# The last output group on one Trainium2 core: both token halves share the first k-tiles, and the accumulators come from another pool

## The chip, the cores and the metric

The kernel runs on one core of one Trainium2 chip. The metric is the device time of one execution in microseconds, as the median of several runs. The profile is that of one more execution; its span is what the profiler saw of it from the first to the last event.

## The reference

One layer of a decoder trunk with three token-mixer branches. What matters here is its end:

```python
merged = (g_sb * (o_sb @ w_branch_sb[layer])
          + g_ssd * (o_ssd @ w_branch_ssd[layer])
          + g_mem * (o_mem @ w_branch_mem[layer]))
x = x + merged @ w_out[layer]
...
return rms_norm(x, final_norm_w)
```

`x` is 256 tokens by 2048 channels in float32, `w_out` is 2048 by 2048. The final norm divides each token's row by the root of the mean of its squares, so no part of a row can be written before all 2048 columns of it are there.

## The kernel before

**Tiles.** The 256 tokens are two halves of 128 (`t` is 0 or 1); the 2048 output columns are four groups of `GW` = 512 (`g` is 0 to 3); the contraction over 2048 is 16 k-tiles of 128 (`NKT`). The transposed `merged` lies in `mT` as a high and a low part (`lh`, `ll`), and each chunk of the weights is split in the same manner: ScalarE rounds `raw` to a high part (line 146), VectorE subtracts that for the low part (line 150). A product is then three matmuls: high by high, high by low, low by high.

**Order.** The instructions of each engine stand in the order in which the program is written; a heap of deferred functions (`defer`, `pump`, `drain`) only decides where in that order the evacuations are written. Each engine works its queue in order and waits at semaphores for the others. The framework sets these waits: for data, and for a buffer of a pool whose former tile has not been read yet.

**The groups 0 to 2** go through `gemm`: an accumulator of two banks (one for each token half) from the pool `psA`, which has two such buffers; chunks of two k-tiles; evacuation by `out_half` (VectorE adds `x`, ScalarE squares and sums, GpSimd multiplies by the norm's weights).

**The group 3** is written out by hand. All its weights are loaded and split first, into tiles that stay (`wlh`, `wll`); then `drain()` writes what is still deferred, among it the evacuation of group 2; then come the products, half 0 in one piece of 512 columns, half 1 in two pieces of 256 (`T`), each piece with its own accumulator:

```python
acc = psA.tile([P, 2, GW], F32, tag="acc", name=nm("acc"),
               bufs=2)[:, 0, 0:cs.stop - cs.start]
...
last_cols(t, cs, acc, xr[:, t])
```

`last_cols` goes over 256 columns at a time: VectorE adds `x` (line 891), ScalarE squares and sums (895), VectorE adds the sum to the row's mean (896) and multiplies by the norm's weights (897). Behind the last columns of a half, `write_out` takes the power -1/2 on GpSimd (901), scales the row in five pieces, three on VectorE (908) and two on ScalarE (910), and sends each piece off (911) on the queue of SyncE or of ScalarE.

**The other pool.** `bank(...)` gives single banks of the pool `psB`, which has four buffers. In this part of the program it last held the transposes of `merged` (`mt`, line 832).

Of the kernel before, what the change touches and what calls it, by code (L numbers as in the profile page):

```python
# [10 lines left out]
F32 = mybir.dt.float32  # L11
# [5 lines left out]
P = 128  # L17
D = 2048
T = 256
NKT = D // P  # L20
GW = 512
# [4 lines left out]
LATE = 3  # L26
WARM = 10
LATE_C = 2
NEG = -1.0e30

SB_HEADS = 8
# [10 lines left out]
def trunk_kernel(  # L42
# [6 lines left out]
    nc = tc.nc  # L49
# [7 lines left out]
    psA = ctx.enter_context(tc.tile_pool(name="psA", bufs=2, space=bass.MemoryType.PSUM))  # L57
# [4 lines left out]
    def nm(s):  # L62
        cnt[0] += 1
        return f"{s}_{cnt[0]}"
# [13 lines left out]
    def tq(shape, n):  # L78
        return tmp.tile(shape, F32, tag="tq", name=nm(n), bufs=2)

    def small(shape, n="small"):
        return sm.tile(shape, F32, tag="small", name=nm(n), bufs=12)
# [4 lines left out]
    def bank(shape, n="bank"):  # L87
        return psB.tile(shape, F32, tag="bank", name=nm(n))
# [19 lines left out]
    def keep_warm(n):  # L108
        for _ in range(n):
# [9 lines left out]
    nc.gpsimd.memset(cmask, 0.0)  # L119
    nc.gpsimd.affine_select(out=smask, in_=cmask, compare_op=ALU.is_gt, fill=NEG, base=0,  # L120
                            pattern=[[1, P]], channel_multiplier=-1)
    nc.gpsimd.affine_select(out=cmask, in_=cmask, compare_op=ALU.is_ge, fill=NEG, base=0,
                            pattern=[[1, P]], channel_multiplier=-1)
# [48 lines left out]
    def defer(fn, chunks=LATE):  # L172

        cnt[0] += 1
        heapq.heappush(late, (now[0] + chunks, cnt[0], fn))
# [9 lines left out]
    def pump():  # L185


        now[0] += 1
        while late and late[0][0] <= now[0]:
            heapq.heappop(late)[2]()  # L190
        advance(lanes[now[0] % 2])
# [6 lines left out]
    def drain():  # L198
        while lanes[0] or lanes[1] or late:
            pump()  # L200
# [10 lines left out]
    def gemm_cols(lhs, nk, w, c0, evac, ready=None, acc=None):  # L211
# [7 lines left out]
        for k0 in range(0, nk, KCC):  # L219
# [16 lines left out]
            pump()  # L236
        defer(lambda: evac(acc), LATE_C)

# [200 lines left out]
    for g in range(4):  # L439
        gemm_cols(memT, NKT, w_mem_kv, 2 * g * P, to_split_cols(kT, 2 * g),  # L440
                  acc=None if g else [bank([P, 2, T], "acc") for _ in range(2)])
# [384 lines left out]
    mT = []  # L826
# [61 lines left out]
    def last_cols(t, cs, acc, xr):  # L888
        for c in range(cs.start, cs.stop, T):
            yc = yo[t][:, 3 * GW + c:3 * GW + c + T]  # L890
            nc.vector.tensor_tensor(yc, acc[:, c - cs.start:c - cs.start + T], xr[:, c:c + T],
                                    ALU.add)
            junk = tq([P, T], "junk")
            q = ssy[:, t, 3 + c // T:4 + c // T]
            nc.scalar.activation(junk, yc, AF.Square, scale=D ** -0.5, accum_out=q)
            nc.vector.tensor_tensor(msy[:, t:t + 1], q, msy[:, t:t + 1], ALU.add)
            nc.vector.tensor_tensor(yc, yc, fw[:, 3 * GW + c:3 * GW + c + T], ALU.mult)

    def write_out(t):
        rs = small([P, 1], "frs")  # L900
        nc.gpsimd.tensor_tensor(rs, msy[:, t:t + 1], mhalf[:, 0:1], ALU.pow)
        for c0, c1, eng, dma in ((0, 256, nc.vector, nc.sync), (256, 640, nc.scalar, nc.scalar),
                                 (640, 1152, nc.vector, nc.sync),
                                 (1152, 1536, nc.scalar, nc.scalar),
                                 (1536, 2048, nc.vector, nc.sync)):
            o = yo[t][:, c0:c1]
            if eng is nc.vector:
                eng.tensor_scalar(o, o, rs, None, ALU.mult)
            else:
                eng.activation(o, o, AF.Copy, scale=rs)  # L910
            dma.dma_start(out[t * P:(t + 1) * P, c0:c1], o)

    def x_chunk(g):
        xr = t4([P, 2, GW], "xr")
        nc.scalar.dma_start(
            xr, x[:, g * GW:(g + 1) * GW].rearrange("(t p) n -> p t n", p=P))
        return xr
# [9 lines left out]
        gemm(mT[0], NKT, w_out, g * GW, out_evac(g))  # L927


    g = 3  # L930
    xr = x_chunk(g)
    his, los = [], []
# [4 lines left out]
        raw = load_chunk(w_out, g * GW, GW, k0, KC)  # L937
        split((his[-1][:, k0 % 4:k0 % 4 + KC], los[-1][:, k0 % 4:k0 % 4 + KC], raw, None))
    drain()
    for t in range(2):  # L940
        tt = slice(t * P, (t + 1) * P)
        for cs in (slice(0, GW),) if t == 0 else (slice(0, T), slice(T, GW)):
            acc = psA.tile([P, 2, GW], F32, tag="acc", name=nm("acc"),
                           bufs=2)[:, 0, 0:cs.stop - cs.start]
            for kt in range(NKT):
                lh, ll = mT[0].at(kt)
                wh, wl = his[kt // 4][:, kt % 4, cs], los[kt // 4][:, kt % 4, cs]
                nc.tensor.matmul(acc, lh[:, tt], wh, start=(kt == 0), stop=False)
                nc.tensor.matmul(acc, lh[:, tt], wl, start=False, stop=False)
                nc.tensor.matmul(acc, ll[:, tt], wh, start=False, stop=(kt == NKT - 1))  # L950
            last_cols(t, cs, acc, xr[:, t])
        write_out(t)


_INS = ['x', 'mem', 'x_cols', 'mem_cols', 'w_cols', 'w_in', 'b_gate', 'dt_bias', 'a_log',
# [39 lines left out]
```

## Time and profile before

| what | value |
|---|---|
| median of 3 runs | 1228.92 us |
| lowest and highest | 1228.18 and 1229.08 us |
| the profiled execution | 1229.58 us |
| its span | 1227.9 us |
| first product of group 3 | 1196.19 us from the span's start |
| last product's end | 1219.84 us |

The profiled execution takes 1.68 us more than its span; that is what lies around the profiled part. Matmuls are pipelined: their starts are closer together than one of them lasts, so the distance between starts is their pace.

### The profile page before, as it was taken

To read this page: it belongs to the slowest core of one execution; us is meant where nothing else is said; L and a number is where in the kernel's file an instruction comes from. 1 tells how busy PE (TensorE), PEld (TensorE's weight loads), DVE (VectorE), ACT (ScalarE), POOL (GpSimd) and SP (SyncE) were. 2 spreads that over 40 slices of the span, in tenths; PEclk is the share of its full clock that TensorE was granted. 3 is DMA by queue.
4 is the path that set the end of the run, shared out by engine and by line. 5 is a ranking of instruction groups with operands and counts; after the bars stand their busy time and mean duration, and the time that the engine had idled before them with its cause. 6 is when DMAs were issued, how large, how long until landed. Compare 5 with 4: busy or idle time off the path is not lost.

```text
span 1227.9 us, 16571 instructions
## 1 busy us (share of the span) xinstructions
PE 1215.4 (99%) x6388; PEld 1034.5 (84%) x6388; DVE 784.5 (64%) x990; ACT 646.0 (53%) x873; POOL 50.9 (4%) x50
## 2 busy tenths in 40 slices
PE   9999999999999999999999999999999999999997
PEld 7888888888888888888888888888878888888886
DVE  5686654565654555888878758577677655555554
ACT  6765444554445454545664756474757544444443
POOL 0000000000000000010100000000000010110101
PEclk9999999999999999999999999999999999999999
DMA  9966566655566656556567666676756666567673
GB/s 333 349 197 188 163 194 189 186 169 166 162 185 181 183 173 187 171 174 179 179 183 225 206 198 219 175 225 188 223 186 186 208 191 210 184 199 242 201 239 112
DMA packets 175023, 242.70 MB, mean 198 GB/s; under 512 B 10272, under 2 KB 109792, under 8 KB 174816
## 3 DMA queue, kind: packets, MB, share of 16 engines
q1 hardware_dynamic: 168224, 229.51, 61.0%
q10 hardware_dynamic: 6720, 12.13, 2.8%
q8 instruction: 50, 0.82, 0.3%
q14 instruction: 29, 0.24, 0.1%
HBM read 239.48 MB, written 2.13 MB: 197 GB/s over the span
## 4 chain that ended last, share of the span: by engine, by line
PE 94%; DMA 2%; ACT 2%; DVE 1%; issue 1%; SPq 0%; POOLq 0%; POOL 0%; ACTq 0%
PE acc L229 29%; PE acc L233 14%; PE acc L266 14%; PE acc L267 14%; PE acc L268 14%; PE acc L398 1%; PE acc L399 1%; PE acc L397 1%; PE y L772 1%; DMA raw<-in_w_branch_sb_dram 1%; DMA raw<-in_w_out_dram 1%; ACT wh L146 1%; DMA raw<-in_w_mem_kv_dram 1%; DVE wl L150 0%; ACT dec L752 0%
## 5 line engine op out<-in xcount | busy, mean ns | idle before, releaser
L150 DVE TENSOR_TENSOR wl<-raw,wh 128x1024 fp32r<-128x1024 f32 (+1 forms) x409 | 504.7, 1237 | 311.3 <-ACT wh L146 305.7
L146 ACT ACTIVATE wh<-raw 128x1024 fp32r<-128x1024 f32 (+1 forms) x409 | 431.1, 1055 | 392.7 <-PE acc L268 200.7
L229 PE MATMUL acc<-hT,wh 128*128 128x512 f32 x1408 | 444.0, 397 | 0.0
L233 PEld LDWEIGHTS acc<-hT,wl 128*128 128x128 f32 x1408 | 264.5, 188 | 62.5
L233 PE MATMUL acc<-hT,wl 128*128 128x256 f32 x1408 | 276.8, 278 | 0.0
L229 PEld LDWEIGHTS acc<-hT,wh 128*128 128x128 f32 x1408 | 214.5, 189 | 0.1
L267 PE MATMUL acc<-wl,hT 128*128 128x512 f32 x448 | 174.8, 390 | 1.4 <-DVE wl L150 1.4
L266 PE MATMUL acc<-wh,hT 128*128 128x512 f32 x448 | 175.8, 392 | 0.0
L268 PE MATMUL acc<-wh,hT 128*128 128x512 f32 x448 | 174.5, 390 | 0.0
L267 PEld LDWEIGHTS acc<-wl,hT 128*128 128x128 f32 x448 | 84.1, 188 | 19.3 <-DVE wl L150 2.3
L266 PEld LDWEIGHTS acc<-wh,hT 128*128 128x128 f32 x448 | 84.1, 188 | 17.7 <-issue 0.7
L268 PEld LDWEIGHTS acc<-wh,hT 128*128 128x128 f32 x448 | 84.1, 188 | 17.6
L266 PE MATMUL acc<-wh,oD 128*128 128x512 f32 x128 | 49.8, 389 | 0.0
L267 PE MATMUL acc<-wl,oD 128*128 128x512 f32 x128 | 49.8, 389 | 0.0
L268 PE MATMUL acc<-wh,oD 128*128 128x512 f32 x128 | 49.8, 389 | 0.0
L687 DVE SCALAR_TENSOR_TENSOR cT<-cu,wcols,cT 128x255 f32<-128x255 f32 (+2 forms) x96 | 46.4, 483 | 3.4
L852 POOL TENSOR_TENSOR merged<-merged,sig 128x512 f32<-128x512 f32 x16 | 24.8, 1572 | 523.7 <-DVE sig L851 523.7
L229 PE MATMUL acc<-memT,wh 128*128 128x512 f32 x128 | 40.5, 398 | 0.0
L266 PE MATMUL acc<-wh,mT 128*128 128x512 f32 x96 | 37.4, 390 | 0.0
L268 PE MATMUL acc<-wh,mT 128*128 128x512 f32 x96 | 37.4, 389 | 0.0
L267 PE MATMUL acc<-wl,mT 128*128 128x512 f32 x96 | 37.4, 389 | 0.0
L630 POOL TENSOR_TENSOR lm<-lm,sp 128x384 f32<-128x384 f32 x8 | 13.1, 1638 | 394.7 <-DVE sp L629 385.0
(250 smaller groups left out, 1297.3 us busy)
## 6 DMA issues: line engine op xcount, KB each, us to landing
raw<-in_w_in_dram SPq DMA_DIRECT2D x288, 512.0 KB, 3.7
raw<-in_w_branch_ssd_dram SPq DMA_DIRECT2D x32, 512.0 KB, 4.1
raw<-in_w_out_dram SPq DMA_DIRECT2D x32, 512.0 KB, 4.9
raw<-in_w_mem_kv_dram SPq DMA_DIRECT2D x31, 512.0 KB, 6.0
raw<-in_w_branch_mem_dram SPq DMA_DIRECT2D x16, 512.0 KB, 3.6
raw<-in_w_branch_sb_dram SPq DMA_DIRECT2D x16, 512.0 KB, 4.9
dec<-acT SPq DMA_DIRECT2D x24, 256.0 KB, 7.7
sig<-in_b_gate_dram ACTq DMA_DIRECT2D x12, 256.0 KB, 4.3
```

Of the source, the lines that this page charges most:

```text
L146: nc.scalar.activation(hi, src, AF.Copy, **({} if scale is None else {"scale": scale}))
L150: nc.vector.tensor_tensor(lo, src, h32, ALU.subtract)
L229: nc.tensor.matmul(halves[b], wh[:, kt - k0, b * P:(b + 1) * P], lhs.both(kt), start=first, stop=False, skip_group_check=True)
L233: nc.tensor.matmul(halves[b][:, 1], wl[:, kt - k0, b * P:(b + 1) * P], lhs.at(kt)[0], start=False, stop=last, skip_group_check=True)
L266: nc.tensor.matmul(a, lh[:, tt], wh[:, j], start=first, stop=False)
L267: nc.tensor.matmul(a, lh[:, tt], wl[:, j], start=False, stop=False)
L268: nc.tensor.matmul(a, ll[:, tt], wh[:, j], start=False, stop=last)
L397: nc.tensor.matmul(a, lh[:, tt], wh[:, g], start=first, stop=False)
L398: nc.tensor.matmul(a, lh[:, tt], wl[:, g], start=False, stop=False)
L630: nc.gpsimd.tensor_tensor(lm, lm, sp, ALU.subtract)
L687: nc.vector.scalar_tensor_tensor(a[:, s:T], u[:, 0:T - s], convw[:, 3 - s, i:i + 1], a[:, s:T], ALU.mult, ALU.add)
L852: nc.gpsimd.tensor_tensor(merged[t][:, cs], merged[t][:, cs], sig[:, t], ALU.add)
```

## The change

Group 3's products are written in another order, and both accumulators are taken from the pool `psB`, one bank of 512 columns for each token half. For the first 8 k-tiles (`BOTH`) the three matmuls of half 0 are followed by the three of half 1, 512 columns each. Then half 0 does its k-tiles 8 to 15, and `last_cols` and `write_out` of half 0 are written. Then half 1 does its k-tiles 8 to 15 for columns 0 to 255, `last_cols` of these, the same for columns 256 to 511, and `write_out`. Nothing else of the kernel is touched; its lines stand one lower.

```diff
+BOTH = 8
...
     drain()
-    for t in range(2):
+
+    accs = [bank([P, GW], "acc") for _ in range(2)]
+
+    def products(t, cs, k0, k1, ends=False):
         tt = slice(t * P, (t + 1) * P)
-        for cs in (slice(0, GW),) if t == 0 else (slice(0, T), slice(T, GW)):
-            acc = psA.tile([P, 2, GW], F32, tag="acc", name=nm("acc"),
-                           bufs=2)[:, 0, 0:cs.stop - cs.start]
-            for kt in range(NKT):
-                lh, ll = mT[0].at(kt)
-                wh, wl = his[kt // 4][:, kt % 4, cs], los[kt // 4][:, kt % 4, cs]
-                nc.tensor.matmul(acc, lh[:, tt], wh, start=(kt == 0), stop=False)
-                nc.tensor.matmul(acc, lh[:, tt], wl, start=False, stop=False)
-                nc.tensor.matmul(acc, ll[:, tt], wh, start=False, stop=(kt == NKT - 1))
-            last_cols(t, cs, acc, xr[:, t])
-        write_out(t)
+        for kt in range(k0, k1):
+            lh, ll = mT[0].at(kt)
+            wh, wl = his[kt // 4][:, kt % 4, cs], los[kt // 4][:, kt % 4, cs]
+            for i, (a, b) in enumerate(((lh, wh), (lh, wl), (ll, wh))):
+                nc.tensor.matmul(accs[t][:, cs], a[:, tt], b, start=(kt == 0 and i == 0),
+                                 stop=(ends and kt == k1 - 1 and i == 2),
+                                 skip_group_check=True)
+
+    everything = slice(0, GW)
+    for kt in range(BOTH):
+        for t in range(2):
+            products(t, everything, kt, kt + 1)
+    products(0, everything, BOTH, NKT, ends=True)
+    last_cols(0, everything, accs[0], xr[:, 0])
+    write_out(0)
+    for cs in (slice(0, T), slice(T, GW)):
+        products(1, cs, BOTH, NKT, ends=True)
+        last_cols(1, cs, accs[1][:, cs], xr[:, 1])
+    write_out(1)
```

How TensorE's order changes at the start of group 3. The rows give line, operation, output and inputs, the output's partitions by columns, and in brackets the engine for whose semaphore the instruction waits. Before, with `acc_10153` for half 0:

```order
L948 MATMUL acc_10153<-wlh_10099,mT_8525 128x512 [waits Activation_49]
L949 MATMUL acc_10153<-wll_10100,mT_8525 128x512 [waits DVE_49]
L950 MATMUL acc_10153<-wlh_10099,mT_8525 128x512
L948 MATMUL acc_10153<-wlh_10099,mT_8525 128x512
L949 MATMUL acc_10153<-wll_10100,mT_8525 128x512
L950 MATMUL acc_10153<-wlh_10099,mT_8525 128x512
```

And of the change, with `acc_10153` for half 0 and `acc_10154` for half 1:

```order
L951 MATMUL acc_10153<-wlh_10099,mT_8525 128x512 [waits PE_49,Activation_49]
L951 MATMUL acc_10153<-wll_10100,mT_8525 128x512 [waits DVE_49]
L951 MATMUL acc_10153<-wlh_10099,mT_8525 128x512
L951 MATMUL acc_10154<-wlh_10099,mT_8525 128x512 [waits PE_49]
L951 MATMUL acc_10154<-wll_10100,mT_8525 128x512
L951 MATMUL acc_10154<-wlh_10099,mT_8525 128x512
```

Half 1's first products moved up between those of half 0; their waits for TensorE itself are for writes in these banks that lie some 440 products back.

TensorE again, where columns 0 to 255 of half 1 end and columns 256 to 511 begin. Before, in two accumulators (`acc_10224`, `acc_10278`):

```order
L948 MATMUL acc_10224<-wlh_10129,mT_8528 128x256
L949 MATMUL acc_10224<-wll_10130,mT_8528 128x256
L950 MATMUL acc_10224<-wlh_10129,mT_8528 128x256
L948 MATMUL acc_10278<-wlh_10099,mT_8525 128x256 [waits DVE_49,PE_49]
L949 MATMUL acc_10278<-wll_10100,mT_8525 128x256
L950 MATMUL acc_10278<-wlh_10099,mT_8525 128x256
```

And of the change, both in `acc_10154`:

```order
L951 MATMUL acc_10154<-wlh_10129,mT_8528 128x256 x2
L951 MATMUL acc_10154<-wll_10130,mT_8528 128x256
L951 MATMUL acc_10154<-wlh_10129,mT_8528 128x256
L951 MATMUL acc_10154<-wlh_10119,mT_8527 128x256 [waits DVE_49]
L951 MATMUL acc_10154<-wll_10120,mT_8527 128x256
```

The wait before was for the first readers of `acc_10153`, whose buffer `acc_10278` takes; that of the change is for another VectorE instruction, the addition of half 1 that stands fourth in the next rows (the number that the wait names is the one that this addition counts up to).

VectorE's order in the change, from `write_out(0)` into `last_cols(1)` (`yo_9616` is the output row block of half 0, `yo_9617` that of half 1):

```order
L909 TENSOR_SCALAR yo_9616<-yo_9616,frs_10237 128x256 [waits Pool_49]
L909 TENSOR_SCALAR yo_9616<-yo_9616,frs_10237 128x512
L909 TENSOR_SCALAR yo_9616<-yo_9616,frs_10237 128x512 [waits DVE_49]
L892 TENSOR_TENSOR yo_9617<-acc_10154,xr_10097 128x256 [waits PE_49]
L897 TENSOR_TENSOR msy<-ssy,msy 128x1 [waits Activation_49]
L898 TENSOR_TENSOR yo_9617<-yo_9617,fw_9618 128x256 [waits DVE_49]
L892 TENSOR_TENSOR yo_9617<-acc_10154,xr_10097 128x256 [waits PE_49]
```

Nothing moved on VectorE: the same instructions stand in the same order before, with the accumulators `acc_10224` and `acc_10278` in the two additions.

## Rows read from the trace of the kernel before

**Rows 1.** From the page: the span, TensorE's busy time, and the chain that ended last by engine.

```profile
span 1227.9 us, 16571 instructions
PE 1215.4 (99%) x6388; PEld 1034.5 (84%) x6388; DVE 784.5 (64%) x990; ACT 646.0 (53%) x873; POOL 50.9 (4%) x50
...
PE 94%; DMA 2%; ACT 2%; DVE 1%; issue 1%; SPq 0%; POOLq 0%; POOL 0%; ACTq 0%
```

**Rows 2.** Who waited for whom from 1185 to 1228 us: us in total, times, longest.

```profile
DVE yo L891 <- PE acc L950: 4.6, 2, 4.2
...
PEld acc L948 <- DVE yo L879: 1.2, 1, 1.2
...
PE acc L948 <- DVE yo L879: 0.8, 1, 0.8
```

**Rows 3.** Timeline of TensorE (PE) in group 3: start, us, line, output and inputs, shape; the idle time before it in brackets. The first and last of half 0 (48 products of 512 columns), the first two of half 1's columns 0 to 255, its last (the 48th), and the last of columns 256 to 511.

```profile
1196.19 0.39 PE L948 MATMUL acc<-wlh,mT 128*128 128x512 f32 x1
...
1206.86 0.39 PE L950 MATMUL acc<-wlh,mT 128*128 128x512 f32 x1
...
1208.06 0.39 PE L948 MATMUL acc<-wlh,mT 128*128 128x256 f32 x1 [0.81 <-DVE yo L879]
...
1208.29 0.28 PE L949 MATMUL acc<-wll,mT 128*128 128x256 f32 x1
...
1213.80 0.28 PE L950 MATMUL acc<-wlh,mT 128*128 128x256 f32 x1
...
1219.56 0.28 PE L950 MATMUL acc<-wlh,mT 128*128 128x256 f32 x1
```

**Rows 4.** Timeline: the last subtraction for `wll` on VectorE (DVE), and the product of half 0 that reads it.

```profile
1204.45 1.22 DVE L150 TENSOR_TENSOR wll<-raw,wlh 128x1024 fp32r<-128x1024 f32 x1 [0.45 <-ACT wlh L146]
...
1205.95 0.40 PE L949 MATMUL acc<-wll,mT 128*128 128x512 f32 x1
```

**Rows 5.** Timeline of VectorE: the last two instructions of group 2's evacuation shown are the addition for half 1 and the mean's step; then `last_cols(0)`, the three scalings of `write_out(0)` merged into one row, and the first addition of half 1.

```profile
1207.33 0.68 DVE L879 TENSOR_TENSOR yo<-acc,xr 128x512 f32<-128x512 f32 x1
...
1208.99 0.15 DVE L886 TENSOR_SCALAR msy<-fs 128x1 f32<-128x1 f32 x1
1209.07 0.42 DVE L891 TENSOR_TENSOR yo<-acc,xr 128x256 f32<-128x256 f32 x1
...
1210.21 0.42 DVE L897 TENSOR_TENSOR yo<-yo,fw 128x256 f32<-128x256 f32 x1
1210.54 0.42 DVE L891 TENSOR_TENSOR yo<-acc,xr 128x256 f32<-128x256 f32 x1
...
1212.55 1.14 DVE L908 TENSOR_SCALAR yo<-yo,frs 128x256 f32<-128x256 f32 x3 [0.45 <-POOL frs L901]
1214.12 0.42 DVE L891 TENSOR_TENSOR yo<-acc,xr 128x256 f32<-128x256 f32 x1 [0.43 <-PE acc L950]
```

**Rows 6.** Timeline of the other engines there: the power on GpSimd (POOL), ScalarE's (ACT) second output transfer of half 0, its square of half 1's columns 0 to 255, and VectorE's steps behind it.

```profile
1211.84 0.67 POOL L901 TENSOR_TENSOR frs<-msy,mhalf 128x1 f32<-128x1 f32 x1 [1.70 <-DVE msy L896]
...
1214.25 0.36 ACTq L911 DMA_DIRECT2D out_dram<-yo  x1
...
1214.66 0.42 ACT L895 ACTIVATE junk<-yo 128x256 f32<-128x256 f32 x1 [0.44 <-DVE yo L891]
...
1215.20 0.16 DVE L896 TENSOR_TENSOR msy<-ssy,msy 128x1 f32<-128x1 f32 x1 [0.65 <-ACT junk L895]
...
1215.28 0.42 DVE L897 TENSOR_TENSOR yo<-yo,fw 128x256 f32<-128x256 f32 x1
```

**Rows 7.** Timeline of the tail: the last addition, and the last output transfer that is issued.

```profile
1219.88 0.42 DVE L891 TENSOR_TENSOR yo<-acc,xr 128x256 f32<-128x256 f32 x1 [4.18 <-PE acc L950]
...
1223.51 0.34 ACTq L911 DMA_DIRECT2D out_dram<-yo  x1
```

**Rows 8.** Stretches: two that hold most of group 3's products, then single microseconds behind the last of them. Columns: length, busy us of PE, PEld, DVE, ACT, POOL (with counts), then TensorE's granted clock as a share of full speed, the DMA engines' busy share and GB/s.

```profile
1196.19:1207.25 11.06, 11.06 (x49) 8.82 (x47) 7.34 (x8) 5.75 (x7) 0.14 (x1) 1.00 0.44 152
...
1213.82:1219.84 6.02, 6.02 (x51) 5.82 (x49) 0.92 (x3) 0.91 (x3) 0.00 (x0) 1.00 0.50 176
...
1220.00:1221.00 1.00, 0.00 (x0) 0.00 (x0) 0.42 (x3) 0.51 (x2) 0.00 (x0) 1.00 0.00 0
...
1223.00:1224.00 1.00, 0.00 (x0) 0.00 (x0) 0.00 (x0) 0.47 (x1) 0.00 (x0) 1.00 0.95 338
1224.00:1225.00 1.00, 0.00 (x0) 0.00 (x0) 0.00 (x0) 0.00 (x0) 0.00 (x0) 0.66 1.00 384
```

**Rows 9.** The DMA engines' busy share, in tenths, from 1190 to 1228 us in 40 slices of 0.95 us. Slices 25 to 28 (from 1213.7) are the output of half 0, slices 34 to 37 (from 1222.3) that of half 1, counted from 0.

```profile
DMA  8997579869793000000000000999100000199800
```

## The prediction

> **What bounds the kernel now.** I read the page first, then the waits of the last 43 us, then the timeline of the last group engine by engine. The page shows one engine as the limit: TensorE is busy for 99% of the span and stands for 94% of the chain that ended last [rows 1]. Only the last 32 us differ between the two kernels, so the views are narrowed to them. Of the waits there, one is TensorE's own: 0.81 us before the first product of token half 1 (the last two rows of the group) [rows 2]. Everything behind TensorE's last product is a serial tail: VectorE's addition of the last quarter starts at 1219.88 and the span ends at 1227.9 [rows 1, 7], 8.02 us in which TensorE does nothing. What counts for the end of the program is therefore one moment: when VectorE begins that last addition (the second `last_cols` of token half 1, columns 256 to 511). Whatever the change does, I take the 8.02 us behind it as they are, and ask where that moment moves.
>
> **Where it lies now.** TensorE does 48 products of 512 columns for half 0: the first starts at 1196.19, the last at 1206.86, so one starts every (1206.86 - 1196.19)/47 = 0.227 us. It then stands until 1208.06, and does 96 products of 256 columns, one every 0.12 us from there on (1213.80 to 1219.56 is 48 of them, 5.76 us). The last ends at 1219.56 + 0.28 = 1219.84 [rows 3], and VectorE starts 0.04 us behind it [rows 7].
>
> **What the change takes away.** Two things on TensorE. First the stand. `acc` of half 1 came out of a pool of two buffers, and the one it was given had still to be read by VectorE for group 2 (the addition at 1207.33, which ends at 1208.01) [rows 2, 5]. The new accumulators are in the other pool, whose buffers were last read by splits of `mT` long before; neither of them waits for group 2. From the pace, the next product would have stood at 1206.86 + 0.227 = 1207.09 rather than 1208.06, so this is 0.97 us. Second, 48 products of 256 columns become 24 of 512: 48 x 0.12 - 24 x 0.227 = 5.76 - 5.45 = 0.31 us. Taken by TensorE alone, the last product would then start at 1196.19 + 72 x 0.227 + 47 x 0.12 = 1218.17 and end at 1218.45: 1.39 us earlier than now.
>
> **What it costs nothing to move.** In the new order each pair of k-tiles is used at a slower pace at first (both halves use it), so the weights have more time. Before, the last subtraction that makes a `wll` ends at 1204.45 + 1.22 = 1205.67 and the product that reads it started at 1205.95 [rows 4]; now the same tile is wanted after 48 + 19 products, at 1196.19 + 67 x 0.227 = 1211.4. The cover is 5.7 us, and the splits themselves wait for loads and for nothing that TensorE does here. The additions, squares and multiplications of group 2 (`out_half`) stay where they were, behind the splits on VectorE, until 1209.1 [rows 5]; nothing of the last group waits for them any more.
>
> **What it moves later, and this is the dear part.** Half 0 now ends not after 48 products but after 72. The last starts at 1196.19 + 71 x 0.227 = 1212.31, ends 0.39 later, and with the same 0.04 VectorE's first addition of half 0 starts at 1212.74 instead of 1209.07: 3.67 us later. Behind it on VectorE stand, in this order and before anything of half 1, the rest of `last_cols(0)` and the three scalings of `write_out(0)`. From the first addition to the first scaling is 1212.55 - 1209.07 = 3.48 us (squares on ScalarE and the power on GpSimd lie in between), and the three scalings take 1.14 [rows 5, 6]. So VectorE has its queue free at 1212.74 + 3.48 + 1.14 = 1217.36; consecutive instructions overlap by 1210.21 + 0.42 - 1210.54 = 0.09 [rows 5], so the next may start at 1217.27. The bounds for that step are 1217.27 and 1217.36; I take the first, which is a pair of rows of the same kind.
>
> The next instruction is the addition for columns 0 to 255 of half 1. Its products are long done: 24 after half 0's last, so their last starts at 1212.31 + 0.227 + 23 x 0.12 = 1215.30 and ends at 1215.58. Before the change the VectorE addition sat 0.43 us waiting for TensorE [rows 5]; now TensorE's result sits 1.69 us waiting for VectorE.
>
> That alone would be harmless, but the order of TensorE's instructions shows a new wait: the first product for columns 256 to 511 of half 1 waits for VectorE. The number it waits for in the built program is the increment of exactly that addition of columns 0 to 255. Both column halves are now in one accumulator tile, one bank, and the addition that reads one half must end before the products that write the other half may start. Before, each column half had a tile of its own, and TensorE ran on from the one half to the other, at one pace from 1213.80 on [rows 3]. So the last 24 products can't start before 1217.27 + 0.42 = 1217.69, plus 0.05 to restart (1208.01 to 1208.06, the old stand) [rows 3, 5], which is 1217.74. From such a restart to VectorE's next addition the trace has one measured case: 1208.06 to 1214.12, 6.06 us for 48 products [rows 3, 5], the slower first one included. With 24 products fewer it is 6.06 - 24 x 0.12 = 3.18. The last addition starts at 1220.92.
>
> In the Trainium skill, "PSUM — Partial Sum Buffer", section "PSUM bank collisions raise a hardware error", says that accesses of two engines are to be kept apart by bank and quadrant and not by address. By that rule the wait belongs there and the sum is the +1.04 below; by addresses alone it would be the -0.60 of the second rival. No stretch of the trace before has two engines at work in one accumulator bank, so the trace neither bears the rule out nor speaks against it.
>
> **The sum.** 1220.92 - 1219.88 = +1.04 us. TensorE does 1.39 us less and is done later, because 2.16 us (1215.58 to 1217.74) of new standing come in. The rest of the tail is as before: squares of columns 0 to 255 are finished on ScalarE well before 1220.92 (it is free of its second output transfer at 1214.25 + 0.36 + 3.67 = 1218.28, and the square and the two small VectorE steps took from 1214.66 to 1215.70 [rows 6]). The output of half 0 moves 3.67 us later: it was on its way in the slices from 1213.7 to about 1217.5 and that of half 1 from 1222.3 on [rows 9]; then it is through by 1221.2, against 1223.3 for half 1. The price of that is nothing, with 2 us to spare. The profiled execution took 1229.58 with a span of 1227.9, so it would be 1228.94 and 1230.62. It lies 0.66 above the median of 1228.92; on the median the same difference gives **1229.96 us**. The runs of before lie between 1228.18 and 1229.08; I hold 0.2%, 2.46 us, to be about what can be told from no change, and +1.04 is under it.
>
> **The rivals.**
> *TensorE's saving comes through whole* (2 in 100). The last product would end at 1218.45 and the addition start at 1218.49, -1.39 us, 1227.5. Against it: VectorE works its queue in order, and the trace shows 4.62 us of `last_cols(0)` and `write_out(0)` between half 0's result and the next addition [rows 5].
> *The new wait doesn't bind* (6 in 100), as if the tile's halves were told apart. Then TensorE is done at 1218.45 but VectorE is not: ScalarE takes up the square of columns 0 to 255 at 1214.66 + 3.67 = 1218.33, the multiplication follows 0.62 later at 1218.95 (1214.66 to 1215.28 [rows 6]), and the last addition 0.33 after that (1210.21 to 1210.54 [rows 5]), at 1219.28. That is -0.60, 1228.3.
> *TensorE's clock falls in the new stand* (5 in 100); this is the one on the far side. The products of the last group ran at a granted clock of 1.00 [rows 8], which is 2.4 GHz. The 24 last ones would take twice 0.12 each at 1.2 GHz, 24 x 0.12 = 2.88 more, +3.92 in all, 1232.8, slower by 0.32%. It decides if the grant is gone when TensorE starts again after 2.16 us. Against it: behind the last product of before (1219.84), the grant still reads 1.00 in each microsecond up to 1224 and 0.66 in the one after that [rows 8]; the new stand is about half as long as that. The skill's page "TensorE: Matmul & The Clock Gate", section "What's actually happening", has the clock return to half speed when the engine idles, which the fall at the end of these rows bears out.
> *The outputs of the two halves collide* (3 in 100): if half 0's output took 2 us longer, the two would share the queues. Half 0's output has 3.8 us of transfer; half of it spilling over would cost at most 1.9 us: +2.9, 1231.9. The gap of 2 us above speaks against it.
>
> **How the numbers follow.** The forecast (+1.04, 1229.96) has 84 in 100. Its own unknowns are small: the overlap on VectorE (0 to +0.09), the restart (0 to 0.1 either way) and the spread of the runs, half a microsecond either way. The range from 1228.8 to 1231.2 takes these in on both sides and leaves out the rivals, the one at 1228.3 by a little more than the runs' spread reaches; it is meant to hold the time 8 times in 10. Faster by over 0.2% (below 1226.5) no mechanism gives, not even the whole saving: 2 in 100. Slower by over 0.2% (above 1231.4) takes the clock or a collision: 6 in 100. In between: 92.
>
> **What would show it.** The profile after should have: no stand of TensorE ahead of the last group's second token half; VectorE's first addition of half 0 at about 1212.7 and its three scalings at about 1216.2; a TensorE wait for VectorE's addition of about 2.2 us between the 24th and 25th of the products of 256 columns; the last addition at about 1220.9 and the same 8 us behind it. I am wrong if TensorE runs through from one column half to the other, if the addition of columns 0 to 255 gets in ahead of the scalings of half 0, or if the granted clock reads less than 1.00 in the last 3 us of products.

## The result, and the profile after

The changed kernel takes **1230.86 us** in the median of 13 runs (1229.82 to 1233.93), the kernel before 1228.92 (13 runs, 1228.05 to 1230.15). Between the two medians lie 1.94 us; the ratio over all the runs is 1.0021, with a 95% interval from 1.0014 to 1.0029: 1.7 to 3.6 us slower. The forecast was +1.04 us and "within 0.2%"; the time is inside the range that was given, but the loss is about twice the forecast one. Three executions further on ran in a slower state and are left out of every comparison: one of the filled kernel (1340.63 us, mean clock 0.85) and two of the kernel before (2471.96 and 3146.12 us).

The profiled execution of the changed kernel took 1230.68 us. Its page, the lines that answer to [rows 1]:

```profile
span 1228.1 us, 16523 instructions
...
PE 1214.1 (99%) x6364; PEld 1032.7 (84%) x6364; DVE 785.1 (64%) x990; ACT 646.1 (53%) x873; POOL 51.0 (4%) x50
...
PE 97%; ACT 1%; issue 1%; DMA 1%; DVE 0%; SPq 0%; POOLq 0%; POOL 0%; ACTq 0%
```

TensorE's busy time is 1.3 us less (1215.4 before). In group 3, from the first product to the last one's end without the stands, it is 1220.04 - 1195.38 - 2.17 = 22.49 us against 1219.84 - 1196.19 - 0.81 = 22.84, so the change gives 0.35 us of that; the rest is in the part ahead, which differs from execution to execution. The span is 0.2 us longer. Who waited for whom from 1185 to 1229 us, which answers to [rows 2]:

```profile
DVE yo L892 <- PE acc L951: 5.3, 2, 3.8
...
PEld acc L951 <- DVE yo L892: 2.4, 1, 2.4
PE acc L951 <- DVE yo L892: 2.2, 1, 2.2
```

The 0.81 us ahead of half 1 are gone; 2.17 us for VectorE's addition of columns 0 to 255 have come (the forecast was 2.16). TensorE's timeline, which answers to [rows 3]: the first product of group 3, half 0's last (a row of two: the second is the first of half 1's columns 0 to 255), the last of columns 0 to 255, and the first and last of columns 256 to 511:

```profile
1195.38 0.39 PE L951 MATMUL acc<-wlh,mT 128*128 128x512 f32 x1
...
1211.47 0.50 PE L951 MATMUL acc<-wlh,mT 128*128 128x512 f32 x2
...
1214.45 0.28 PE L951 MATMUL acc<-wlh,mT 128*128 128x256 f32 x1
1216.90 0.38 PE L951 MATMUL acc<-wlh,mT 128*128 128x256 f32 x1 [2.17 <-DVE yo L892]
...
1219.76 0.28 PE L951 MATMUL acc<-wlh,mT 128*128 128x256 f32 x1
```

And VectorE's, which answers to [rows 5, 7]: the first addition of half 0, the three scalings of `write_out(0)`, and the two additions of half 1:

```profile
1211.90 0.42 DVE L892 TENSOR_TENSOR yo<-acc,xr 128x256 f32<-128x256 f32 x1 [3.79 <-PE acc L951]
...
1215.37 1.14 DVE L909 TENSOR_SCALAR yo<-yo,frs 128x256 f32<-128x256 f32 x3 [0.45 <-POOL frs L902]
1216.43 0.42 DVE L892 TENSOR_TENSOR yo<-acc,xr 128x256 f32<-128x256 f32 x1
...
1220.08 0.42 DVE L892 TENSOR_TENSOR yo<-acc,xr 128x256 f32<-128x256 f32 x1 [1.56 <-PE acc L951]
```

In this execution everything ahead of group 3, which the change doesn't touch, happened to be 0.81 us quicker (1195.38 against 1196.19 in [rows 3]). So the two spans can't be set against each other; the stretch from group 3's first product to the last addition can. It was 1219.88 - 1196.19 = 23.69 us and is 1220.08 - 1195.38 = 24.70: **+1.01**, against +1.04 in the sum. Behind the last addition the span goes on for 8.02 us, as before. The granted clock in this execution, to be read beside [rows 8], is 1.00 through the stand and the products behind it:

```profile
1214.73:1216.90 2.17, 0.00 (x1) 0.00 (x0) 1.67 (x5) 1.09 (x2) 0.61 (x1) 1.00 0.12 42
1216.90:1220.04 3.14, 3.13 (x24) 2.93 (x24) 0.50 (x2) 0.65 (x3) 0.00 (x0) 1.00 0.86 305
```

So the trace shows one microsecond, and the runs two or more. The 13 runs aren't alike: seven have spans from 1228.1 to 1229.1, six from 1230.2 to 1231.5, and the mean granted clock of the first is 0.998 (one of them 0.997), of the second 0.996 (one of them 0.997). The experiments had to tell where the second microsecond is.

### The profile page after: what moved, and what is told of

The parts are those of the page before. It is cut to its first block, busy times and chain, and to the rows that moved or that the text cites. A ratio compares the mean times of both kernels' runs of the same rounds, so it can differ in the third digit from the quotient of the medians.

```text
span 1228.1 us, 16523 instructions
## 1 busy us (share of the span) xinstructions
PE 1214.1 (99%) x6364; PEld 1032.7 (84%) x6364; DVE 785.1 (64%) x990; ACT 646.1 (53%) x873; POOL 51.0 (4%) x50
## 4 chain that ended last, share of the span: by engine, by line
PE 97%; ACT 1%; issue 1%; DMA 1%; DVE 0%; SPq 0%; POOLq 0%; POOL 0%; ACTq 0%
PE acc L230 29%; PE acc L267 15%; PE acc L268 15%; PE acc L269 15%; PE acc L234 14%; PE acc L951 1%; PE acc L399 1%; PE acc L400 1%; PE acc L398 1%; PE y L773 1%; DMA raw<-in_w_mem_kv_dram 1%; PE dtp L460 0%; DVE wl L151 0%; PE xp L731 0%; PE mt L833 0%
```

## The experiments

Two theories stood against each other. **Clock:** the stand costs 1.0 us in every execution; in some, the granted clock falls at or behind it and the last 24 products take up to 2 us more. **Spread:** the clock has no part in it, and the changed kernel loses time elsewhere or in a way no trace would show. All times are against the kernel before on the same chip, whose medians there were 1228.66 to 1229.16; banks of their own, the shorter stand, the pool alone the second time and both cures ran on one chip, the others on another.

**The changed kernel once more** (no edit).

> The changed kernel once more. Theory (clock): the new stand of TensorE ahead of half 1's last 24 products is 2.2 us in every execution and costs about 1.0 us; in part of the executions (about half, as in the first 13) the granted clock falls at or behind that stand, and these take 2.5 to 2.9 us more, so that the times fall into two groups, near +1.0 to +1.4 us and near +3.9 us against before. A trace that catches one of the second group shows products of 256 columns 0.24 apart. Rival (spread of the chip): the times lie evenly between +0.5 and +4, and no trace shows the last products at another pace than 0.12.

Measured: 1230.74 in the median of 11 runs, ratio 1.0013 (1.0004 to 1.0022). The trace is of the quick kind again: the same 24.70 us from first product to last addition, all products at a grant of 1.00. Two times stand apart from the others, 1232.58 and 1232.66, with mean clocks of 0.997 and 0.996. Two kinds again, with the slower one rarer than the half that was expected, and +3.4 us where +3.9 was; nothing of the cause yet.

**The stand filled.**

```diff
+    fill = bank([P, T], "fill")
     for cs in (slice(0, T), slice(T, GW)):
         products(1, cs, BOTH, NKT, ends=True)
+        if cs.start == 0:
+            for _ in range(15):
+                nc.tensor.matmul(fill, mT[0].at(0)[0][:, 0:P], his[0][:, 0, 0:T],
+                                 start=True, stop=True)
```

> The changed kernel with 15 products of 256 columns put into the stand, into a bank that nothing reads; they add work but nothing waits for them (15 x 0.12 = 1.8 us of 2.17). Clock theory: the wait for VectorE stays where it is and the last addition still comes 1.0 us later than before, but every execution is of the first group: median +1.0 us against before, highest below +2.5, granted clock 0.998 in all. Rival: as the changed kernel, +1.9 in the median with single times up to +5.

Measured: median 1230.06, ratio 1.0004 (0.9995 to 1.0013), mean +0.94 us; the ten times compared lie between 1229.58 and 1230.78, and none of their mean clocks is under 0.998. The interval doesn't exclude that the kernel takes as long as before; the trace shows the microsecond. Its timeline: the 15 fillers, the first product behind the stand, and VectorE's last addition:

```profile
1214.75 1.96 PE L968 MATMUL fill<-wlh,mT 128*128 128x256 f32 x15
1217.08 0.39 PE L952 MATMUL acc<-wlh,mT 128*128 128x256 f32 x1 [0.37 <-DVE yo L893]
```

```profile
1220.26 0.42 DVE L893 TENSOR_TENSOR yo<-acc,xr 128x256 f32<-128x256 f32 x1 [1.56 <-PE acc L952]
```

The first product of group 3 is at 1195.55, so the stretch is 24.71 us: the wait for VectorE is as long as in the changed kernel, only TensorE isn't idle in it. With more work and the same wait, the slower kind of execution is gone. That speaks for the clock; with ten times, where the unfilled kernel beside it had two of over 1232 in eleven, it is not proof by itself.

**An execution of the slower kind, caught** (no edit, three single executions).

> The changed kernel, one look, in search of an execution of the slower group. Clock theory: a third to a half of such looks have a span over 1230; in these the granted clock reads less than 1.00 between 1215 and 1222 and the last 24 products of 256 columns lie up to 0.24 apart; the others read 1.00 until the last product and 0.12. Rival: a look with a span over 1230 shows the last products 0.12 apart and loses its time elsewhere.

> As the look before it: the changed kernel once more; clock theory, in a third to a half of the looks the last 24 products run at half clock and the span is over 1230; rival, no look shows the last products at another pace than 0.12.

> As the two looks before it: the changed kernel once more; clock theory, in a third to a half of the looks the last 24 products run at half clock and the span is over 1230; rival, no look shows the last products at another pace than 0.12.

Measured: 1230.88, 1230.33 and 1229.21. The second and third are of the quick kind (stands of 2.18 and 2.17 us, a grant of 1.00 throughout). The first is the one looked for; its span is 1229.2 and not over 1230 as expected, because here too the part ahead of group 3 was quick (first product at 1194.97). The granted clock in single microseconds, with the columns of [rows 8]:

```profile
1215.00:1216.00 1.00, 0.00 (x0) 0.00 (x0) 1.00 (x3) 0.58 (x1) 0.00 (x0) 1.00 0.00 0
1216.00:1217.00 1.00, 0.50 (x3) 0.51 (x4) 0.44 (x2) 0.61 (x1) 0.00 (x0) 0.93 0.78 279
1217.00:1218.00 1.00, 1.00 (x7) 1.00 (x6) 0.39 (x2) 0.51 (x2) 0.00 (x0) 0.50 1.03 383
...
1219.00:1220.00 1.00, 1.00 (x6) 1.00 (x6) 0.00 (x0) 0.00 (x0) 0.00 (x0) 0.50 0.12 40
1220.00:1221.00 1.00, 1.00 (x9) 0.92 (x7) 0.00 (x0) 0.00 (x0) 0.00 (x0) 0.87 0.00 0
1221.00:1222.00 1.00, 0.12 (x2) 0.00 (x0) 0.42 (x1) 0.38 (x2) 0.00 (x0) 1.00 0.00 0
```

The grant is 1.00 all through the stand and drops to 0.50, the 1.2 GHz level, a few tenths of a microsecond after the products have started again; it comes back within 1220 to 1221, with products running all the time since 1216.50. The products behind the stand on TensorE, and the last addition on VectorE:

```profile
1214.04 0.28 PE L951 MATMUL acc<-wlh,mT 128*128 128x256 f32 x1
1216.50 0.39 PE L951 MATMUL acc<-wlh,mT 128*128 128x256 f32 x1 [2.18 <-DVE yo L892]
...
1217.24 0.41 PE L951 MATMUL acc<-wll,mT 128*128 128x256 f32 x1
...
1217.88 0.41 PE L951 MATMUL acc<-wll,mT 128*128 128x256 f32 x1
...
1220.37 0.28 PE L951 MATMUL acc<-wll,mT 128*128 128x256 f32 x1
...
1220.85 0.28 PE L951 MATMUL acc<-wlh,mT 128*128 128x256 f32 x1
```

```profile
1221.16 0.42 DVE L892 TENSOR_TENSOR yo<-acc,xr 128x256 f32<-128x256 f32 x1 [3.05 <-PE acc L951]
```

From 1217.24 to 1217.88 are three products, 0.213 us each where the other executions have 0.12. From the restart to the addition are 1221.16 - 1216.50 = 4.66 us, against 1220.08 - 1216.90 = 3.18 in the profile after: 1.48 us for the clock. The whole stretch is 1221.16 - 1194.97 = 26.19 us, 2.50 more than before. That is the slower kind, seen once; where the grant is low for all 24 products it would be, as an estimate from these two paces, 24 x (0.213 - 0.12) = 2.2 us.

Taken together, the 27 executions of the changed kernel (13, 11 and the three single ones) sort by their mean granted clock: 16 with 0.998 take 1230.21 us in the mean, 7 with 0.996 take 1232.41, and 4 with 0.997 take 1232.08. The kernel before takes 1229.24 in the mean of 75 executions beside the experiments, on both chips. So it is +1.0 without the fall and +3.2 to +2.8 with it. The class of 0.997 is not clean, since a fall right behind the last product alone can make it, as the run with banks of their own shows below. By their times, two of the four belong to the quick kind (1230.79 and 1231.02) and two to the slower (1232.58 and 1233.93). A mean that rounds to 0.996 is under 0.9965; with the low level at half of full speed it takes at least 2 x 0.0035 x 1230 = 8.6 us at that level, and behind the last product lie only 8.1. Ahead of group 3 the grant reads 1.00 in every trace here. So in these seven executions the grant was most likely low for some time between group 3's first product and its last.

**A longer stand.**

```diff
-BOTH = 8
+BOTH = 12
```

> The changed kernel with BOTH at 12 in place of 8: half 0 ends 12 products later, half 1 has 12 products of 256 columns left for each column half in place of 24. Theory of the stand: VectorE's addition of columns 0 to 255 comes 2.7 us later again and TensorE stands 3.6 us ahead of the last 12 products; the last addition starts 2.3 us later than before. Clock theory: after a stand of that length the last 12 products run at half clock in most executions, 0.24 apart, up to 1.4 us more: median +3 to +4 us against before. Rival (no clock): +2.3 in all executions, products 0.12 apart.

Measured: median 1232.80, ratio 1.0033 (1.0022 to 1.0044), mean clocks of 0.995 to 0.997 in all eight. The stand is 3.61 us, as worked out. TensorE's first product behind it, the last but one, and the clock, in its trace:

```profile
1221.38 0.39 PE L951 MATMUL acc<-wlh,mT 128*128 128x256 f32 x1 [3.61 <-DVE yo L892]
...
1222.67 0.38 PE L951 MATMUL acc<-wll,mT 128*128 128x256 f32 x1
```

```profile
1221.00:1222.00 1.00, 0.62 (x5) 0.62 (x6) 0.32 (x1) 0.56 (x2) 0.00 (x0) 1.00 0.91 323
1222.00:1223.00 1.00, 1.00 (x10) 0.97 (x8) 0.50 (x2) 0.47 (x2) 0.00 (x0) 0.85 1.01 380
```

Here the grant fell only when the products had been running again for more than a microsecond, and hit the last two of twelve. Six of the eight mean clocks are 0.996 or less, which agrees with a fall ahead of the last product in most executions; that the products run slow from the start does not agree with this trace. The stretch is 1223.30 - 1197.13 = 26.17, +2.48 against +2.3 expected. The median is 4.1 us above that of before, just over the +3 to +4 expected, and the interval (+2.7 to +5.4) leaves the size of the clock's part open.

**`write_out(0)` later.**

```diff
     last_cols(0, everything, accs[0], xr[:, 0])
-    write_out(0)
     for cs in (slice(0, T), slice(T, GW)):
         products(1, cs, BOTH, NKT, ends=True)
         last_cols(1, cs, accs[1][:, cs], xr[:, 1])
+        if cs.start == 0:
+            write_out(0)
```

> The changed kernel with write_out of half 0 written behind the first last_cols of half 1. Theory: the stand is long because VectorE's addition of columns 0 to 255 is queued behind the scalings of half 0; freed of them it starts 2.9 us after half 0's first addition instead of 4.5, TensorE stands about 0.6 us instead of 2.17, the last addition starts 0.5 to 0.6 us earlier than before, and no execution has a fallen clock: median -0.5 us against before. Rival (the shared bank itself is what costs): stand and time stay at about +1.

Measured: median 1228.66, ratio 0.9996 (0.9987 to 1.0006), mean -0.53 us; no clock under 0.998. VectorE's order is the new one, and TensorE's stand is 0.58 us:

```profile
1215.52 0.42 DVE L892 TENSOR_TENSOR yo<-acc,xr 128x256 f32<-128x256 f32 x1
...
1216.98 1.14 DVE L909 TENSOR_SCALAR yo<-yo,frs 128x256 f32<-128x256 f32 x3
1219.16 0.42 DVE L892 TENSOR_TENSOR yo<-acc,xr 128x256 f32<-128x256 f32 x1 [1.04 <-PE acc L951]
```

```profile
1215.99 0.38 PE L951 MATMUL acc<-wlh,mT 128*128 128x256 f32 x1 [0.58 <-DVE yo L892]
```

The stretch is 1219.16 - 1196.06 = 23.10: -0.59, where -0.56 was worked out. With the same shared bank the loss is gone and the stretch is shorter than before, so the bank alone does not cost: what costs is the bank together with the queue ahead of its reader.

**Banks of their own for half 1's column halves.**

```diff
-    accs = [bank([P, GW], "acc") for _ in range(2)]
+    acc0 = bank([P, GW], "acc")
+    acc1 = [bank([P, T], "acc") for _ in range(2)]
...
-        for t in range(2):
-            products(t, everything, kt, kt + 1)
+        products(0, everything, kt, kt + 1)
+        for cs in (slice(0, T), slice(T, GW)):
+            products(1, cs, kt, kt + 1)
```

> The changed kernel with a bank for each column half of half 1 (its first 8 k-tiles as products of 256 columns, 0.3 us more work for TensorE). Theory: without the shared bank TensorE has no stand; the last addition is then held by VectorE's and ScalarE's queues (6.54 us behind half 0's first addition, as the second rival of the prediction worked out) and starts 0.3 us earlier than before: median -0.3, no execution with a mean clock under 0.998. Rival (the order alone costs, whatever the banks): +1 or more.

Measured: median 1228.83, ratio 0.9996 (0.9987 to 1.0005), mean -0.43. TensorE has no stand; the last addition starts 23.45 us behind the first product, -0.24, and it is VectorE that is late:

```profile
1217.82 0.42 DVE L892 TENSOR_TENSOR yo<-acc,xr 128x256 f32<-128x256 f32 x1
...
1219.83 0.42 DVE L892 TENSOR_TENSOR yo<-acc,xr 128x256 f32<-128x256 f32 x1
```

TensorE's last product, and the microsecond in which its grant falls:

```profile
1218.72 0.28 PE L952 MATMUL acc<-wlh,mT 128*128 128x256 f32 x1
```

```profile
1221.00:1222.00 1.00, 0.00 (x0) 0.00 (x0) 0.55 (x2) 0.23 (x1) 0.68 (x1) 0.68 0.01 3
```

There is no idle time ahead of the last addition, though TensorE ended at 1219.00 (1218.72 + 0.28). It comes 1219.83 - 1213.29 = 6.54 us behind half 0's first addition, which is the second rival of the prediction, as a kernel. Half 1's column halves have here both a tile and a bank of their own; no run tells whether the wait in the changed kernel is set for the shared tile or for the shared bank. One expectation was missed: four of the eleven have a mean clock of 0.997. They are not slower than the others (1228.39 to 1229.96). In the trace, whose mean is 0.997 too, the grant reads 1.00 until the last product and falls in the microsecond from 1221, so the mean of the whole span there counts only the idle tail. A mean of 0.997 is therefore no proof of a fall that costs.

**A shorter stand.**

```diff
-BOTH = 8
+BOTH = 4
```

> The changed kernel with BOTH at 4: half 0 ends 12 products earlier, VectorE is through with it 2.7 us earlier, while half 1's columns 0 to 255 have 36 products left. Theory: TensorE stands about 0.7 us at the shared bank, the last addition starts 0.2 us earlier than before, no execution with a mean clock under 0.998: median -0.2. Rival (any wait at the shared bank brings the clock down in a part of the executions): single times 1.5 to 2.2 us above the others.

Measured: median 1228.90, ratio 0.9997 (0.9988 to 1.0006), mean -0.40; a stand of 0.73 us, a stretch of 1219.96 - 1196.55 = 23.41 (-0.28), no clock under 0.998. The wait at the shared bank and the last addition:

```profile
1215.35 0.39 PE L951 MATMUL acc<-wlh,mT 128*128 128x256 f32 x1 [0.73 <-DVE yo L892]
```

```profile
1219.96 0.42 DVE L892 TENSOR_TENSOR yo<-acc,xr 128x256 f32<-128x256 f32 x1 [2.99 <-PE acc L951]
```

In eleven executions this shorter wait at the same bank brought no fall.

**The pool alone, twice.**

```diff
-            acc = psA.tile([P, 2, GW], F32, tag="acc", name=nm("acc"),
-                           bufs=2)[:, 0, 0:cs.stop - cs.start]
+            acc = bank([P, cs.stop - cs.start], "acc")
```

This is the kernel before with only its three accumulators moved.

> One part of the change alone: the order of the products as before, only the three accumulators of group 3 from the pool of the background. Theory: the stand of 0.81 us ahead of half 1 is gone, TensorE runs from the first to the last product of group 3 at its pace, and the last addition starts 0.97 us earlier: -1.0 us against before. Rival (VectorE's or ScalarE's queue takes the gain): the last addition moves by less than 0.3 us.

> Once more the order of before with the accumulators from the other pool, for its size: -0.97 us by the theory, as its first trace showed for the last addition (no stand of TensorE in group 3); rival: no difference from before that holds up, under 0.3 us.

Measured: medians 1228.40 and 1227.71, ratios 0.9992 (0.9983 to 1.0001) and 0.9986 (0.9977 to 0.9995). No matmul of group 3 waits any more (in the second trace one weight load waits 0.20 us for the last `wll`). The last additions of the two traces, the first product being at 1196.28 and 1195.85:

```profile
1218.87 0.42 DVE L891 TENSOR_TENSOR yo<-acc,xr 128x256 f32<-128x256 f32 x1 [3.75 <-PE acc L949]
```

```profile
1218.50 0.42 DVE L891 TENSOR_TENSOR yo<-acc,xr 128x256 f32<-128x256 f32 x1 [2.32 <-PE acc L949]
```

Stretches of 22.59 and 22.65, -1.10 and -1.04 (-0.97 was worked out); the mean times are 0.80 and 1.54 us under those of before. The first interval just includes no difference, the second does not, and both traces show the microsecond. This half of the change is a gain, by a short edit: a version faster than both kernels, by about 0.1%.

**Both cures at once**, banks of their own and `write_out(0)` behind the first `last_cols` of half 1 (the two diffs above together).

> Both cures at once: banks of their own for half 1's column halves, and write_out of half 0 written behind the first last_cols of half 1. Theory: TensorE runs through, VectorE is free when its last product ends; the last addition starts 1.07 us earlier than before: median -1.0. Rival: what the tail gains is given back by ScalarE's transfers of half 0's output next to half 1's: -0.5 or less.

Measured: median 1228.08, ratio 0.9989 (0.9980 to 0.9997), stretch 1218.39 - 1195.74 = 22.65 (-1.04):

```profile
1218.39 0.42 DVE L892 TENSOR_TENSOR yo<-acc,xr 128x256 f32<-128x256 f32 x1 [0.20 <-PE acc L952]
```

It equals the pool alone. With TensorE running through, the new order of the products gains nothing more here: the 0.31 us that 24 wider products of half 1 save is given up again where the banks are parted.

## Why the prediction was right and wrong

**The mechanism held, step by step.** In the changed kernel: VectorE's first addition of half 0 lies 1211.90 - 1195.38 = 16.52 us behind the first product (forecast 1212.74 - 1196.19 = 16.55); the stand is 2.17 (2.16); from the restart to the last addition are 3.18 (3.18); the sum is +1.01 (+1.04). The other three traces of the quick kind and that of the filled kernel give 24.69 to 24.71 us for the stretch of 24.70, and the 16 executions with a mean clock of 0.998 lie 0.97 us above the kernel before. The wait that the order showed is real, and TensorE's saving of 1.39 us (most of it the old stand of 0.97; the work itself is 0.35 us less, where 0.31 was worked out) is lost in it: the late addition is queued behind `write_out(0)`, as the run with that moved shows.

**The step that failed is the third rival, the clock.** It was given 5 in 100 and its cost left out of the sum, and it came in 7 to 11 of 27 executions (nine, if the four of 0.997 are told apart by their times). Its place was right (the stand) and its decision point was named (whether the grant is gone when TensorE starts again). What failed is the argument against it: "behind the last product of before, the grant still reads 1.00 in each microsecond up to 1224 ... the new stand is about half as long as that". That was one execution, and it was taken for a fixed delay. In other traces the grant falls sooner or later than that: after the last product at 1220.04 of the profile after, it is already 0.83 in the microsecond from 1222; in the run of the changed kernel once more, whose last product ended at 1219.90, it is 0.50 from 1222 on; with the stand filled and the last product's end at 1220.22, it is still 1.00 up to 1225. In this order:

```profile
1222.00:1223.00 1.00, 0.00 (x0) 0.00 (x0) 0.97 (x3) 0.62 (x1) 0.00 (x0) 0.83 0.00 0
```

```profile
1222.00:1223.00 1.00, 0.00 (x0) 0.00 (x0) 1.00 (x3) 0.58 (x2) 0.00 (x0) 0.50 0.00 0
```

```profile
1225.00:1226.00 1.00, 0.00 (x0) 0.00 (x0) 0.00 (x0) 0.00 (x0) 0.00 (x0) 0.74 1.01 378
```

The shortest of these delays is under 2.1 us (1219.90 to 1222), no longer than the new stand. And the decision point was too narrow: in the caught execution the grant was still there at the restart and went a few tenths later, at the cost of 1.48 us. The prediction's own last sign of being wrong, a grant under 1.00 in the last 3 us of products, names what is seen there.

**Sizes.** The rival's price was put at 24 x 0.12 = 2.88 us, from twice the pace. The measured pace at the low level is 0.213, so all 24 products cost 2.2, and the caught fall, whose grant came back before the end, 1.48. The mean over the 27 executions, 1231.06, is 1.8 us above the 1229.24 of before: 1.0 from the stand, and the rest from the 7 to 11 executions with the fall, about 2.1 us each over eleven. That is close to what all 24 products at the low level would cost; whether the executions without a trace lost all of it there isn't shown. The median of 13 fell on the slowest of the seven quick executions, and that it lies inside the range is luck: with one of the seven over 1231 it would have been 1231.98. The ratio of all runs, +1.7 to +3.6 us, counts both kinds. The forecast also held that 2.46 us is about what can be told from no change; the interval of these 13 runs, 1.8 us wide, told less from it.

**The other rivals.** TensorE's saving through whole: fell, as said. No binding of the wait: fell for this kernel, and its price (-0.60 with one bank) came out as -0.24 where the banks were parted at 0.3 us more work; the 6.54 us from half 0's first addition to the last one, of which it was made, came out exactly. A collision of the outputs: none in the trace; half 0's transfers end before 1220 and half 1's begin at 1223.

**What stays open:** why the grant falls behind the stand in some executions and not in others that are alike in every row up to it. The runs show how often and at what price, and that with work in the stand ten executions had none; nothing in them decides when. The Trainium skill, "TensorE: Matmul & The Clock Gate", section "What's actually happening", says that the chip judges TensorE's activity in windows that run free of the kernel, by which the same stand could be seen differently from one execution to the next. No run here shows that, though the two kinds of execution would agree with it.

## What to carry to other kernels

An accumulator split by columns so that one part can be read early must, in a program like this one, have a tile and bank for each part, or its reader must stand early in its engine's queue; otherwise the next products wait for everything queued ahead of that reader (2.17 us here, 0.58 with the reader moved forward, none with the banks parted). A stand of two microseconds on an engine that otherwise never stops is to be priced twice, once as idle time and once as a chance that the products behind it run at half clock. And where parts of a change can be had apart, cost them apart: here, by the stretches of the traces, the pool was worth -1.0 us and the order with its shared bank +2.0 on top of it, before the clock.

## What the runs showed of the hardware that was not expected

- Three microseconds of products at half clock after a stand of 2.18 us, beginning when TensorE was already at work again (the grant reads 0.93 from 1216 to 1217 and 0.50 from 1217). With 1.96 us of that stand filled by products, none of ten executions had a mean clock under 0.998.
- Of 27 executions of one program, 7 have a mean clock of 0.996 and 16 of 0.998, with 2.2 us between their mean times. A median over few runs moves with the share of the kinds.
- The part ahead of group 3, the same instructions in all of these kernels, ended between 1194.80 and 1197.13 us in the traces. Two single spans can't tell a microsecond; a stretch between two rows of the same trace could: it was 24.69 to 24.71 us in the five traces with the same wait and no fall.
